# Transposes for the next stage's operand: 32x32 blocks turned on VectorE at full height, quadrants permuted through device memory

## The chip, the core and the metric

The kernel runs on one core of a Trainium2 chip. The metric is device microseconds of one execution, from the first to the last instruction with what the runtime adds around them. TensorE (PE) does matmuls and transposes into PSUM, VectorE (DVE) and ScalarE (ACT) do elementwise work, GpSimd (POOL) some small things, SyncE (SP) starts the loads.

## The reference, cut to what matters

Two layers of an encoder on 256 tokens of width 2048, all in float32. Each layer is three residual steps, each with an RMSNorm ahead:

```
for i in range(2):
    h = h + (even_mixer if i == 0 else odd_mixer)(h, ...)   # norm, projections, attention, projection
    h = h + swiglu(rmsnorm(h), w_gate, w_up, w_down)        # 2048 -> 5632 -> 2048
    h = h + (p[i] @ w_proj) * sigmoid(rmsnorm(h) @ w_pg)    # per-layer embedding
return rmsnorm(h)
```

The even mixer joins a sparse attention over chosen keys with gated linear attention; the odd one is stick-breaking attention with 16 heads of 128. Every product `rmsnorm(h) @ W` contracts over the 2048 columns of `h`, so the 256 tokens of `h` are needed with their columns along the partitions, that is transposed. The same holds for the hidden values of the feed-forward (5632 columns) and for q and k of the odd mixer.

## The kernel before

`h` stays in SBUF as 128 partitions x 2 halves of the tokens x 2048 columns. A product streams its weights once: a unit (`unit`, L176) loads four chunks of 128 rows by 512 columns, 1 MB, in one DMA begun by SP (L184) into one of two `raw` buffers. In two half units each (two chunks), ScalarE casts them to float32r (`whi`, L99), VectorE subtracts to get the low part (`wlo`, L100), each into one of four buffers, and PE does 12 matmuls: for each chunk and each half of the tokens high x high (L201), high x low (L202) and low x high (L203). `block` (L206) runs four units for a contraction of 2048 and leaves two PSUM tiles of 128x512, one for each half of the tokens.

Everything that isn't the stream of weights is put into a list by `later` (L161). `tick` (L169), called after each half unit, takes at most one entry from its front once the entry's delay in half units has gone by and, if it names another entry with `after`, so many half units after that one; `need` (L165) empties the list up to an entry at once. So the order of writing weaves this work into the stream. The framework then plans an order of instructions for each engine from the written order and its own times; in the trace an instruction can stand ahead of one written earlier. Each engine runs its own order strictly, and each queue of DMA issues too.

Three kinds of transposes are in the kernel.

1. The next operand. When a column block of 512 of `h` is final, `finish_cols` (L224) squares it for the norm and puts two calls of `turn_h` (L135) into the list. Each does four 128x128 transposes on PE into a PSUM tile (L141); ScalarE multiplies by the norm's gain and rounds (L146), VectorE forms the low part (L147). The next stage's first block asks for two chunks each with `need`. This happens for five norms, four column blocks each, two calls per block. A sixth norm, the first, is turned while x arrives (`arrive`, L239).
2. The hidden values of the feed-forward (`ffn`, L782): each of 11 blocks of 512 in each of two layers is turned by `turn_blocks` (L123), four list entries of four VectorE transposes each, 32 partitions x 256 columns (L128), into `hx`; then `split_hid` casts (L789) and subtracts (L790).
3. q and k of the odd mixer (`odd_mixer`, L690): the same `turn_blocks`, straight into `qT` and `kT`, four groups of heads, two each. `scores` (L701) then multiplies them on PE (L709, L711); `shares` and `sums` follow.

Other names: `ple` (L847) is the embedding step, `gated` (L861) its sigmoid, product and sum; it begins with four short blocks of two chunks. For the last quarter of the last embedding step `keep` (L892) loads half-wide weights into a buffer of its own (`kept`) and splits them ahead of time. `mixer_out` (L674) is the projection behind a mixer; `square_sum` (L105) writes its squares, which nobody reads, into `sqs`. `stage` (L55) is one buffer for small loads and constants. The final stage sends `h` out (L934).

Of the kernel before, what the change touches and what calls it, by code (L numbers as in the profile page):

```python
# [27 lines left out]
def trunk_kernel(ctx: ExitStack, tc: tile.TileContext, x, p, even_norm, even_w_in, even_w_gk,  # L28
# [36 lines left out]
    # the activation tables and the tensor engine's clock are up when the data comes  # L65
# [7 lines left out]
    # norm gains, one row of 128 per chunk, turned so that a chunk's gains lie along the partitions  # L73
# [29 lines left out]
    ss = {}  # L103

    def square_sum(key, tt, cb, src):  # L105
        if key not in ss:
            ss[key] = sm.tile([P, NT, 4], F32, name="ss")
        scr = sm.tile([P, NB], F32, name="sqs", bufs=1)
        nc.scalar.activation(scr, src, AF.Square, accum_out=ss[key][:, tt, cb:cb + 1])
# [25 lines left out]
    def turn_h(dst, norm, c2):  # L135
        """Chunks 2*c2 and 2*c2+1 of h, transposed, times the gain, split."""
# [39 lines left out]
    def unit(ps, stat, k0, cols, first, last, nk=KU, kw0=None, step=KU, pre=None):  # L176
        """nk chunks of the contraction: cols = [(weight, first column, width)]."""
# [28 lines left out]
    def block(stat, cols, nk=KC, key=None, ps=None, k0=0, k1=None, kw=0, pre=None):  # L206
        """Output columns over chunks k0..k1 of the contraction; returns the two PSUM tiles."""
# [43 lines left out]
    with tc.issue_after(got_gains.ins):  # L251
# [4 lines left out]
    # upb[s, c] = 1/16 where s <= c in one chunk of 64; sub[s, c] = 1/16 where s > c there  # L256
    upb = const.tile([P, P], F32, name="upb")
    nc.gpsimd.memset(upb, 0.0625)
    nc.gpsimd.affine_select(upb, upb, pattern=[[1, P]], compare_op=OP.is_ge, fill=0.0, base=0,
                            channel_multiplier=-1)  # L260
    nc.gpsimd.memset(upb[0:64, 64:128], 0.0)
    sub = stage("sub")[:, :P]
    nc.gpsimd.memset(sub, 0.0625)
    nc.gpsimd.affine_select(sub, sub, pattern=[[-1, P]], compare_op=OP.is_gt, fill=0.0, base=0,
                            channel_multiplier=1)
    nc.gpsimd.memset(sub[64:128, 0:64], 0.0)
    subr = const.tile([P, P], F32R, name="subr")
    nc.vector.tensor_copy(subr, sub)
    # keys no later than the query, in one chunk
    upm = upb.bitcast(I32)  # L270
    # strictly earlier keys, keys along the partitions
# [8 lines left out]
    # -1 where the first index is no earlier than the second  # L280
# [10 lines left out]
    def even_mixer(xs, ps0, ep):  # L291
# [3 lines left out]
        oT = new_act()  # L295

# [12 lines left out]
        def tokens(ps, name, w=NB):  # L309
            """The block's last w columns by tokens, scaled by the row's norm."""  # L310
# [7 lines left out]
        # u0: c (128), the last pair of q_idx (128), k_idx (64), zeros (64), k_idx again (64),  # L318
        # the gate's low-rank part (16), one
# [6 lines left out]
        # c and three pairs of q_idx  # L326
# [8 lines left out]
        # a pair of q_idx, k_idx, w_idx and the gate's low-rank part  # L335
# [71 lines left out]
        def index_heads(pairs, tt):  # L407
            """pairs: [(the pair's columns by tokens, its first head)]"""
# [45 lines left out]
        def choose(tt, n):  # L454
            """Rounds 2n and 2n+1 of eight best each, for 64 in all."""
# [527 lines left out]
```

## Time and profile before

| | |
|---|---|
| time, median of 3 runs | 2442.11 us (2441.62 to 2442.64) |
| span of the profiled execution | 2438.5 us |
| PE busy | 2417.6 us, 99% |
| VectorE busy | 1506.6 us, 62% |
| ScalarE busy | 1154.1 us, 47% |
| GpSimd busy | 19.2 us, 1% |
| weight loads | 447 MB, 184 GB/s over the span |

The span is the profiled execution's own time, from its first to its last instruction. Busy times come from that execution; matmuls overlap, so the time that one adds is read from the starts of its neighbours and not from its own duration. A wait is read from the idle time of an engine just before an instruction and from what ended it.

### The profile page before, as it was taken

The numbers are of one execution on the slowest core, as the hardware profiler recorded it, in microseconds if no ns is written. First come the engines' busy times: TensorE is split into PE (matmuls) and PEld (weight loads), VectorE is DVE, ScalarE is ACT, GpSimd is POOL, SyncE is SP. The second block draws the span as 40 slices with busy tenths as digits, with TensorE's granted clock in tenths as the row PEclk, the third lists the DMA queues.
The fourth block names the chain that finished last, engine by engine and source line by source line (L and its number), as shares of the span: only waits on it lengthen the run. The fifth ranks groups of instructions, "written<-read, shape, count | busy, mean of one in ns | idle before, by whom it ended". The sixth has DMA issues, their size and how long they took to land.

```text
span 2438.5 us, 27647 instructions
## 1 busy us (share of the span) xinstructions
PE 2417.6 (99%) x10966; PEld 1996.5 (82%) x10966; DVE 1506.6 (62%) x1907; ACT 1154.1 (47%) x1418; POOL 19.2 (1%) x45
## 2 busy tenths in 40 slices
PE   8999999999999999999999999999999999999998
PEld 7887788888888888888888888888888888888887
DVE  5765555766756665655676666557667556556564
ACT  6644444344434434446546565544444344444463
POOL 0000000000000000000000000000000000000000
PEclk9999999999999999999999999999999999999999
DMA  6454455566556565555554454555655655556563
GB/s 211 147 169 151 144 194 186 189 196 201 189 192 193 186 205 183 198 190 185 178 190 156 161 184 165 180 190 177 203 190 192 205 190 186 196 187 206 182 231 123
DMA packets 231651, 450.01 MB, mean 185 GB/s; under 512 B 9457, under 2 KB 16337, under 8 KB 231394
## 3 DMA queue, kind: packets, MB, share of 16 engines
q1 hardware_dynamic: 231234, 447.07, 55.6%
q8 instruction: 86, 1.41, 0.2%
q10 hardware_dynamic: 288, 1.18, 0.1%
q14 instruction: 43, 0.35, 0.0%
HBM read 446.12 MB, written 2.10 MB: 184 GB/s over the span
## 4 chain that ended last, share of the span: by engine, by line
PE 91%; issue 5%; ACT 2%; DVE 1%; DMA 1%; SPq 0%; POOLq 0%; POOL 0%; DVEq 0%; ACTq 0%
PE mm L202 29%; PE mm L201 29%; PE mm L203 29%; PE at L141 1%; DVE kT L128 1%; DVE wlo L100 0%; DMA raw<-in_odd_w_in_dram 0%; PE at L424 0%; DMA h<-in_x_dram 0%; PE at L742 0%; DVE sp L719 0%; ACT whi L99 0%; ACT sp L716 0%; ACT sp L715 0%; ACT L715 0%
## 5 line engine op out<-in xcount | busy, mean ns | idle before, releaser
L100 DVE TENSOR_TENSOR wlo<-raw,whi 128x1024 fp32r<-128x1024 f32 (+2 forms) x848 | 1020.7, 1213 | 794.1 <-ACT whi L99 790.1
L99 ACT CAST whi<-raw 128x1024 fp32r<-128x1024 f32 (+2 forms) x848 | 874.8, 1042 | 1053.5 <-PE mm L203 668.8
L201 PE MATMUL mm<-whi,aH 128*128 128x512 f32 (+2 forms) x2656 | 1036.9, 390 | 0.7 <-ACT whi L99 0.7
L202 PE MATMUL mm<-wlo,aH 128*128 128x512 f32 (+2 forms) x2656 | 1028.8, 387 | 4.1 <-DVE wlo L100 4.1
L203 PE MATMUL mm<-whi,aL 128*128 128x512 f32 (+2 forms) x2656 | 1028.7, 387 | 0.0
L202 PEld LDWEIGHTS mm<-wlo,aH 128*128 128x128 f32 x2656 | 499.4, 188 | 104.7 <-DVE wlo L100 5.9
L203 PEld LDWEIGHTS mm<-whi,aL 128*128 128x128 f32 x2656 | 499.1, 188 | 103.4 <-issue 1.0
L201 PEld LDWEIGHTS mm<-whi,aH 128*128 128x128 f32 x2656 | 499.2, 188 | 102.9 <-issue 2.8
L201 PE MATMUL mm<-whi,hH 128*128 128x512 f32 x704 | 277.2, 394 | 0.0
L202 PE MATMUL mm<-wlo,hH 128*128 128x512 f32 x704 | 277.0, 393 | 0.0
L203 PE MATMUL mm<-whi,hL 128*128 128x512 f32 x704 | 273.6, 389 | 0.0
L128 DVE STREAM_TRANSPOSE hx<-sl 32x256 f32<-32x256 f32 x352 | 153.6, 436 | 6.1
L201 PEld LDWEIGHTS mm<-whi,hH 128*128 128x128 f32 x704 | 132.2, 188 | 30.0
L203 PEld LDWEIGHTS mm<-whi,hL 128*128 128x128 f32 x704 | 132.2, 188 | 29.7
L202 PEld LDWEIGHTS mm<-wlo,hH 128*128 128x128 f32 x704 | 132.4, 188 | 26.1
L146 ACT ACTIVATE aH<-at,gT 128x256 fp32r<-128x256 f32 x96 | 45.1, 473 | 51.4 <-DVE aL L147 47.5
L789 ACT CAST hH<-hx 128x1024 fp32r<-128x1024 f32 x22 | 23.2, 1054 | 92.6 <-DVE hx L128 92.6
L147 DVE SCALAR_TENSOR_TENSOR aL<-at,gT,aH 128x256 fp32r<-128x256 f32 x96 | 45.8, 480 | 22.0 <-ACT aH L146 21.9
L234 DVE TENSOR_TENSOR h<-mm,h 128x512 f32<-128x512 f32 x80 | 52.4, 682 | 2.7 <-PE mm L203 2.7
L141 PE MATMUL at<-ident,h 128*128 128x128 f32 x192 | 30.5, 283 | 5.0 <-DMA h<-in_x_dram 5.0
L141 PEld LDWEIGHTS at<-ident,h 128*128 128x128 f32 x192 | 24.9, 145 | 11.8 <-DMA h<-in_x_dram 3.0
L128 DVE STREAM_TRANSPOSE qT<-tok 32x256 f32<-32x256 f32 x64 | 27.9, 436 | 6.8 <-ACT tok L762 5.8
(221 smaller groups left out, 806.8 us busy)
## 6 DMA issues: line engine op xcount, KB each, us to landing
raw<-in_ffn_w_gate_dram SPq DMA_DIRECT2D x88, 1024.0 KB, 5.2
raw<-in_ffn_w_up_dram SPq DMA_DIRECT2D x88, 1024.0 KB, 5.2
raw<-in_ffn_w_down_dram SPq DMA_DIRECT2D x88, 1024.0 KB, 5.0
raw<-in_odd_w_in_dram SPq DMA_DIRECT2D x48, 1024.0 KB, 5.2
raw<-in_even_w_in_dram SPq DMA_DIRECT2D x36, 1024.0 KB, 5.0
raw<-in_ple_w_gate_dram SPq DMA_DIRECT2D x28, 1024.0 KB, 5.1
raw<-in_even_w_out_dram SPq DMA_DIRECT2D x16, 1024.0 KB, 5.1
raw<-in_odd_w_out_dram SPq DMA_DIRECT2D x16, 1024.0 KB, 5.0
```

Source lines behind the costliest of these rows:

```text
L99: nc.scalar.copy(hi, raw)
L100: nc.vector.tensor_tensor(lo, raw, hi.bitcast(F32), OP.subtract)
L128: nc.vector.transpose(dst[32 * a:32 * a + 32, :, :, 32 * q:32 * q + 32], src.rearrange("p t (m a c) -> p t m a c", a=4, c=32)[32 * q:32 * ...
L141: nc.tensor.transpose(ps[:, c, tt, :], h[:, tt, k * P:(k + 1) * P], ident)
L146: nc.scalar.activation(dst[0][:, k, :], src, AF.Copy, scale=g)
L147: nc.vector.scalar_tensor_tensor(dst[1][:, k, :], src, g, dst[0][:, k, :].bitcast(F32), op0=OP.mult, op1=OP.subtract)
L201: nc.tensor.matmul(ps[tt][:, :n], sh, hi[:, c, :n], start=st, stop=False)
L202: nc.tensor.matmul(ps[tt][:, :n], sh, lo[:, c, :n], start=False, stop=False)
L203: nc.tensor.matmul(ps[tt][:, :n], sl, hi[:, c, :n], start=False, stop=en)
L234: nc.vector.tensor_tensor(hs, ps[tt], hs, OP.add)
L789: nc.scalar.copy(d[0], t)
```

## The change

`turn_blocks` is gone; `turn_h` stays for the first norm only. In their place stands `cross`. It turns a block of 256 tokens by 512 columns with one VectorE instruction over all 128 partitions, which transposes each 32x32 block where it lies. Then whole quadrants of 32 partitions must change places with groups of columns. For that four DMAs begun by GpSimd write the four quadrants (32 partitions, 128 KB each, in runs of 1 KB) into a tile in device memory, and two DMAs, also begun by GpSimd, read it back, one for each half of the tokens (128 partitions, 256 KB, in runs of 512 bytes). A read needs all four writes. The tile that comes back, `tx`, has two buffers, so has the one in device memory, and the one between has one.

All five later norms use it: `finish_cols` puts `cross` into the list and two half units behind it two calls of `gain_h`, which multiplies and splits from `tx` as `turn_h` did from PSUM. The feed-forward puts `cross` and, two half units behind it, `split_hid`, which reads `tx` in permuted order. In the odd mixer a ScalarE copy from `tx` into `qT` or `kT` follows two half units behind, and the layout of these two goes by heads.

Room in SBUF is made for it: `sqs` shares the buffer of `stage`; `sgm` is gone, so `gated` writes the sigmoid into its PSUM tile, takes the product into the embedding's tile and adds that; the kept weights are loaded into the two `raw` buffers; the constants `upb` and `subr` move into the even mixer's pool; and `mixer_out` is split in two, so that the pool of `cross` opens when that of the even mixer closes.

```diff
     def square_sum(key, tt, cb, src):
...
-        scr = sm.tile([P, NB], F32, name="sqs", bufs=1)
+        scr = sm.tile([P, NB], F32, name="sqs", tag="stage", bufs=1)
...
-    def turn_blocks(dst, src, a):
...
+    def cross(src):
...
+        tq = pools["x"].tile([P, 4, NT, 4, 32], F32, name="tq", bufs=1)
+        nc.vector.transpose(tq.rearrange("p a t m r -> p t m a r"),
+                            src.rearrange("p t (m a c) -> p t m a c", a=4, c=32))
+        x = pools["x"].tile([P, 8, 4, 32], F32, name="tx")
+        y = pools["y"].tile([4, 32, 4, NT, P], F32, name="ty")
         for q in range(4):
-            nc.vector.transpose(dst[32 * a:32 * a + 32, :, :, 32 * q:32 * q + 32],
-                                src.rearrange("p t (m a c) -> p t m a c", a=4, c=32)[32 * q:32 * q + 32, :, :, a, :])
+            nc.gpsimd.dma_start(y[:, :, q].rearrange("a c t n -> c a (t n)"),
+                                tq[32 * q:32 * q + 32].rearrange("c a t m r -> c a (t m r)"))
+        for t in range(NT):
+            nc.gpsimd.dma_start(x[:, 4 * t:4 * t + 4].rearrange("p q m r -> p q (m r)"),
+                                y[:, :, :, t].rearrange("a c q n -> (a c) q n"))
+        return x
+
+    def crossed(x):
...
+        return x.rearrange("p q m r -> p m q r")
+
+    def flat(t):
...
+        return t.rearrange("p m (q r) -> p m q r", q=8)
...
+    def gain_h(dst, norm, x, c2):
...
+        for k in (2 * c2, 2 * c2 + 1):
+            g = gT[1][:, (norm - 1) * KC + k:(norm - 1) * KC + k + 1]
+            src = crossed(x)[:, k % 4]
+            hi, lo = (flat(d[:, k:k + 1, :])[:, 0] for d in dst)
+            nc.scalar.activation(hi, src, AF.Copy, scale=g)
+            nc.vector.scalar_tensor_tensor(lo, src, g, hi.bitcast(F32), op0=OP.mult, op1=OP.subtract)
...
     def finish_cols(nx, cb):
...
+        x = {}
+        first = (nx["key"], "x", cb)
+        later(lambda: x.update(x=cross(h[:, :, cb * NB:(cb + 1) * NB])), key=first)
         for c2 in (2 * cb, 2 * cb + 1):
-            later(lambda c2=c2: turn_h(nx["dst"], nx["norm"], c2), key=(nx["key"], c2))
+            later(lambda c2=c2: gain_h(nx["dst"], nx["norm"], x["x"], c2), key=(nx["key"], c2), after=(first, 2))
...
-                nc.tensor.matmul(pz[:, 0:256], kT[:, 0, js], qT[:, :, js], start=True, stop=False,
+                nc.tensor.matmul(pz[:, 0:256], kT[:, j, 0:P], qT[:, j, :], start=True, stop=False,
                                  skip_group_check=True)
-                nc.tensor.matmul(pz[:, 256:384], kT[:, 1, js], qT[:, 1, js], start=False, stop=False,
+                nc.tensor.matmul(pz[:, 256:384], kT[:, j, P:], qT[:, j, P:], start=False, stop=False,
                                  skip_group_check=True)
...
-                for a in range(4):
-                    later(lambda t=t, d=dst, a=a: turn_blocks(d.rearrange("p t (m c) -> p t m c", c=P), t, a))
+                x = {}
+                later(lambda t=t, x=x: x.update(x=cross(t)), key=("x3", g, i))
+                later(lambda d=dst, x=x: nc.scalar.copy(flat(d), crossed(x["x"])), after=(("x3", g, i), 2))
                 T.append(dst)
...
-        def split_hid(dst, t, k0):
-            d = [dst[n][:, k0:k0 + 4, :] for n in range(2)]
-            nc.scalar.copy(d[0], t)
-            nc.vector.tensor_tensor(d[1], t, d[0].bitcast(F32), OP.subtract)
+        def split_hid(dst, x, k0):
+            hi, lo = (flat(dst[n][:, k0:k0 + 4, :]) for n in range(2))
+            nc.scalar.copy(hi, crossed(x))
+            nc.vector.tensor_tensor(lo, crossed(x), hi.bitcast(F32), OP.subtract)
...
-                hx = fp.tile([P, 4, NT * P], F32, name="hx")
-                for a in range(4):
-                    later(lambda d=hx, t=sl, a=a: turn_blocks(d.rearrange("p m (t c) -> p t m c", t=NT), t, a))
-                later(lambda t=hx, n=n, gi=gi: split_hid(hT[gi], t, 4 * n), key=("hT", i, b))
+                x = {}
+                later(lambda t=sl, x=x: x.update(x=cross(t)), key=("xT", i, b))
+                later(lambda x=x, n=n, gi=gi: split_hid(hT[gi], x["x"], 4 * n), key=("hT", i, b),
+                      after=(("xT", i, b), 2))
...
-            sgm = pp.tile([P, NB], F32, name="sgm", bufs=2)[:, :w]
-            nc.scalar.activation(sgm, pg[:, :w], AF.Sigmoid, scale=rs[:, tt:tt + 1])
-            nc.vector.tensor_tensor(sgm, sgm, eb[c0 // NB][tt][:, c0 % NB:c0 % NB + w], OP.mult)
...
+            nc.scalar.activation(pg[:, :w], pg[:, :w], AF.Sigmoid, scale=rs[:, tt:tt + 1])
+            e = eb[c0 // NB][tt][:, c0 % NB:c0 % NB + w]
+            nc.vector.tensor_tensor(e, pg[:, :w], e, OP.mult)
             hs = h[:, tt, c0:c0 + w]
-            nc.vector.tensor_tensor(hs, hs, sgm, OP.add)
+            nc.vector.tensor_tensor(hs, hs, e, OP.add)
...
-            raw = pp.tile([P, KU, HB], F32, name="kept", bufs=1)
+            raw = wp.tile([P, KU, NB], F32, name="raw", bufs=2)[:, :, :HB]
```

## Rows read from the trace of the kernel before

**Rows 1.** which engine is busy; the page's line 1, busy us, share, instructions

```profile
span 2438.5 us, 27647 instructions
PE 2417.6 (99%) x10966; PEld 1996.5 (82%) x10966; DVE 1506.6 (62%) x1907; ACT 1154.1 (47%) x1418; POOL 19.2 (1%) x45
```

**Rows 2.** busy time by windows: the first feed-forward, the odd mixer

```profile
440.00:1080.00 640.00, 640.00 (x2816) 528.34 (x2816) 399.86 (x460) 266.64 (x269) 0.00 (x0) 1.00 0.59 194
1215.00:1560.00 345.00, 341.14 (x1561) 283.12 (x1560) 229.88 (x332) 195.70 (x244) 0.70 (x1) 1.00 0.52 172
```

**Rows 3.** waits of PE, the longest one that isn't at the start

```profile
PE mm L202 <- DVE wlo L100: 4.1, 5, 0.8
```

**Rows 4.** PE in order of time around one call of turn_h: start, us, instruction

```profile
1082.46 0.39 PE L203 MATMUL mm<-whi,hL 128*128 128x512 f32 x1
1082.69 0.60 PE L141 MATMUL at<-ident,h 128*128 128x128 f32 x4
...
1083.60 0.39 PE L203 MATMUL mm<-whi,hL 128*128 128x512 f32 x1
...
1084.28 0.39 PE L203 MATMUL mm<-whi,hL 128*128 128x512 f32 x1
```

**Rows 5.** groups by line and shape: count, busy us, mean ns, idle before

```profile
L100 DVE TENSOR_TENSOR wlo<-raw,whi 128x1024 fp32r<-128x1024 f32 x832 | 1010.4, 1223 | 779.8 <-ACT whi L99 775.9
L99 ACT CAST whi<-raw 128x1024 fp32r<-128x1024 f32 x832 | 865.5, 1050 | 1040.2 <-PE mm L203 661.2 <-DMA raw<-in_ffn_w_up_dram 152.9 <-DMA raw<-in_odd_w_in_dram 68.9
...
L128 DVE STREAM_TRANSPOSE hx<-sl 32x256 f32<-32x256 f32 x352 | 153.6, 436 | 6.1
...
L146 ACT ACTIVATE aH<-at,gT 128x256 fp32r<-128x256 f32 x96 | 45.1, 473 | 51.4 <-DVE aL L147 47.5 <-PE at L141 3.9
...
L141 PE MATMUL at<-ident,h 128*128 128x128 f32 x192 | 30.5, 283 | 5.0 <-DMA h<-in_x_dram 5.0
...
L733 DVE TENSOR_TENSOR at<-at,diagb 128x256 f32<-128x256 f32 x16 | 6.4, 423 | 0.0
...
L667 POOL TENSOR_TENSOR sg<-sg,gn 128x512 f32<-128x512 f32 x4 | 5.1, 1294 | 5.9 <-ACT sg L665 5.9
```

**Rows 6.** DMA issues: count, KB each, median us from issue to landing

```profile
raw<-in_ffn_w_gate_dram SPq DMA_DIRECT2D x88, 1024.0 KB, 5.2
...
kept<-in_ple_w_gate_dram SPq DMA_DIRECT2D x4, 512.0 KB, 6.0
...
out_dram<-h SPq DMA_DIRECT2D x8, 256.0 KB, 2.8
...
praw<-in_p_dram SPq DMA_DIRECT2D x2, 256.0 KB, 5.1
```

**Rows 7.** SP in order of time, one issue: start, us

```profile
2343.85 0.37 SPq L894 DMA_DIRECT2D kept<-in_ple_w_gate_dram  x1
```

**Rows 8.** all engines in order of time, end of the first embedding step

```profile
1212.27 1.05 ACT L99 CAST whi<-raw 128x1024 fp32r<-128x1024 f32 x1 [1.66 <-PE mm L203]
...
1214.27 1.37 ACT L864 ACTIVATE sgm<-mm,rstd 128x512 f32<-128x512 f32 x2 [0.94 <-PE mm L203]
...
1216.28 1.29 DVE L867 TENSOR_TENSOR h<-h,sgm 128x512 f32<-128x512 f32 x2
```

**Rows 9.** the same, odd mixer, from the end of k to its scores

```profile
1259.30 1.31 ACT L762 ACTIVATE tok<-mm,rstd 128x512 f32<-128x512 f32 x2 [0.54 <-PE mm L203]
...
1260.64 3.57 DVE L128 STREAM_TRANSPOSE kT<-tok 32x256 f32<-32x256 f32 x8 [0.62 <-ACT tok L762]
...
1276.05 0.59 PE L709 MATMUL at<-qT,kT 128*128 128x256 f32 x2
```

**Rows 10.** ScalarE in order of time, last embedding step

```profile
2349.24 1.04 ACT L99 CAST wh<-kept 128x1024 fp32r<-128x1024 f32 x1
2353.91 2.01 ACT L99 CAST whi<-raw 128x1024 fp32r<-128x1024 f32 x2 [3.62 <-DMA raw<-in_ple_w_gate_dram]
...
2358.59 1.05 ACT L99 CAST wh<-kept 128x1024 fp32r<-128x1024 f32 x1
```

More of the change, by code (lines that the diff above doesn't have):

```diff
@@ L121, in rstd_of @@
         return rstds[key]
-    def turn_blocks(dst, src, a):
-        for q in range(4):
-            nc.vector.transpose(dst[32 * a:32 * a + 32, :, :, 32 * q:32 * q + 32],
-                                src.rearrange("p t (m a c) -> p t m a c", a=4, c=32)[32 * q:32 * q + 32, :, :, a, :])
+    pools = {}
+    def cross(src):
[4 more added lines that the diff above has]
+        y = pools["y"].tile([4, 32, 4, NT, P], F32, name="ty")
+        for q in range(4):
+            nc.gpsimd.dma_start(y[:, :, q].rearrange("a c t n -> c a (t n)"),
[8 more added lines that the diff above has]
+        return t.rearrange("p m (q r) -> p m q r", q=8)
     def new_act():
@@ L253, in trunk_kernel @@
     done.update((("n0", i), 0) for i in range(KC // 2))
[L257 to L270, printed above, removed]
     diag = const.tile([P, P], F32, name="diag")
@@ L295, in even_mixer @@
         oT = new_act()
+        upb = ep.tile([P, P], F32, name="upb", bufs=1)
+        nc.gpsimd.memset(upb, 0.0625)
+        nc.gpsimd.affine_select(upb, upb, pattern=[[1, P]], compare_op=OP.is_ge, fill=0.0, base=0,
+                                channel_multiplier=-1)
+        nc.gpsimd.memset(upb[0:64, 64:128], 0.0)
+        sub = stage("sub")[:, :P]
+        nc.gpsimd.memset(sub, 0.0625)
+        nc.gpsimd.affine_select(sub, sub, pattern=[[-1, P]], compare_op=OP.is_gt, fill=0.0, base=0,
+                                channel_multiplier=1)
+        nc.gpsimd.memset(sub[64:128, 0:64], 0.0)
+        subr = ep.tile([P, P], F32R, name="subr", bufs=1)
+        nc.vector.tensor_copy(subr, sub)
+        upm = upb.bitcast(I32)
         def t2(name, dt=F32):
@@ L623, in outputs @@
             for a in range(2):
-                scr = sm.tile([P, NB], F32, name="sqs", bufs=1)
+                scr = sm.tile([P, NB], F32, name="sqs", tag="stage", bufs=1)
                 nc.scalar.activation(scr[:, :256], ov[g][:, tt, a * 256:(a + 1) * 256], AF.Square,
@@ L672, in even_mixer, with mixer_out_first, mixer_out @@
         return oT
-    def mixer_out(oT, W, nx):
+    def mixer_out_first(oT, W):
         for i in range(4):
             need(("oT", i))
-        part = {}
-        for cb in range(2):
-            part[cb] = block(oT, [(W, cb * NB, NB)], k1=8)
+        part = [block(oT, [(W, cb * NB, NB)], k1=8) for cb in range(2)]
         for i in range(4, 8):
             need(("oT", i))
+        return part
+    def mixer_out(oT, W, nx, part):
         for cb in range(4):
-            ps = block(oT, [(W, cb * NB, NB)], ps=part.get(cb), k0=8 if cb < 2 else 0)
+            ps = block(oT, [(W, cb * NB, NB)], ps=part[cb] if cb < 2 else None, k0=8 if cb < 2 else 0)
             add_to_h(ps, cb)
@@ L758, in odd_mixer @@
                     nc.vector.tensor_scalar(rq, rs, float(128 ** -0.5), None, op0=OP.mult)
-                dst = op.tile([P, NT, NB], F32, name="qT" if i == 0 else "kT")
+                dst = op.tile([P, 4, NT * P], F32, name="qT" if i == 0 else "kT")
                 t = op.tile([P, NT, NB], F32, name="tok")
@@ L885, in squared @@
             c0, w = parts[n]
-            scr = sm.tile([P, NB], F32, name="sqs", bufs=1)
+            scr = sm.tile([P, NB], F32, name="sqs", tag="stage", bufs=1)
             nc.scalar.activation(scr[:, :w], h[:, tt, c0:c0 + w], AF.Square, scale=float(D ** -0.5),
@@ L939, in trunk_kernel @@
         nx = start_norm("n1", 1)
-        mixer_out(oT, even_w_out[0], nx)
+        part = mixer_out_first(oT, even_w_out[0])
+    pools["x"] = ctx.enter_context(tc.tile_pool(name="xp", bufs=2))
+    pools["y"] = ctx.enter_context(tc.tile_pool(name="yp", bufs=2, space=bass.MemoryType.DRAM))
+    mixer_out(oT, even_w_out[0], nx, part)
     with tc.tile_pool(name="fp0", bufs=2) as fp:
@@ L950, in trunk_kernel @@
         nx = start_norm("n4", 4)
-        mixer_out(oT, odd_w_out[0], nx)
+        mixer_out(oT, odd_w_out[0], nx, mixer_out_first(oT, odd_w_out[0]))
     with tc.tile_pool(name="fp1", bufs=2) as fp:
```

## The prediction

> **What bounds the kernel now.** I read the busy shares first, then the windows, then the waits. TensorE (PE) is busy 2417.6 of 2438.5 us [rows 1]. Two of its phases are in the windows: in 440 to 1080 us, all feed-forward, it is busy 640.00 of 640 us with 2816 matmuls, so one starts every 0.227 us; in the odd mixer (1215 to 1560) it idles 3.9 us [rows 2]. PE's own waits say the same: the longest group, for the low halves of the weights, is 4.1 us in all [rows 3]. So what counts is (a) work taken off PE, and (b) waits that come to stand in PE's order. VectorE (62%) and ScalarE (47%) matter only through (b). One half unit of weights is 12 matmuls, 12 x 0.227 = 2.73 us; I use it as a clock. The median, 2442.1, is 3.6 us above the span of the profiled execution, and I keep that 3.6.
>
> **The change part by part.**
>
> *Transposes leave PE.* Of the 48 calls of `turn_h`, eight are for the first norm and stay; five norms x 8 = 40 go, with four transposes each. Their 283 ns apiece overlap and are no price [rows 5]. The price is what the matmuls slip: around one call, from the L203 at 1082.46 to the next L203 at 1083.60 is 1.14 us, while three steps without transposes (1083.60 to 1084.28) take 0.68 [rows 4]. So a call costs 0.46 us of PE, and 40 give 18.2 us. PE is full there, so this comes off the end: **-18.2**.
>
> *VectorE.* Gone are 480 transposes of 32x256 (30 blocks x 16) at 436 ns, 209 us [rows 5]. Each of 50 crossings (20 for norms, 8 in the odd mixer, 22 in the feed-forwards) adds one of 128x1024. No such one is in the trace. A 32x256 one takes about what a two-input instruction of 128x256 takes (423 ns), and a two-input one of 128x1024 takes 1223 ns; bounds 1.2 and 4 x 0.436 = 1.74 us; I take 1.23, as the 256-wide shapes agree [rows 5]. VectorE ends 148 us less busy. Nothing waits for it but in the odd mixer, where its stretches of transposes delay the weights' low halves; of the 3.9 us idle there [rows 2] I give back **-2** (bounds 0 and -3.9). ScalarE gets eight copies of 128x1024 more, 1.05 us each like its casts [rows 5].
>
> *The chain of a crossing.* Transpose, four writes of 128 KB begun by GpSimd, a wait of its queue for all four, two reads of 256 KB, arrival. GpSimd starts no DMA in the trace, so I bound by other queues' rows: 256 KB of output reach memory in 2.8 us, 256 KB in rows of 1 KB arrive in 5.1 us, 512 KB of them in 6.0 [rows 6]. For an issue I take 0.4 us, as SP takes (0.37 [rows 7]); GpSimd's longest instructions, 1.29 us [rows 5], are the other end. Middle: 1.23 + 4 x 0.4 + 2.8 + 2 x 0.4 + 5.1 = 11.5 us. High: 1.74 + 4 x 1.3 + 2.8 + 2 x 1.3 + 6.0 = 18.3. Low: 1.2 + 1.6 + 1.4 + 0.8 + 2.8 = 7.8, each write being half of the output's row and a read as quick as that.
> The Trainium skill ("DMA: Bandwidth & Descriptors", Anatomy of one DMA — SWDGE path) gives a DMA begun by GpSimd about 2.0 us plus its bytes at 436 GB/s; by it, estimated, write and read would land in 2.3 and 2.6 us and the chain would take 8.5 us; the sum would be 1.7 us lower. The trace of before has no such DMA to hold against it.
>
> *Who waits for it: next stages.* The last column block's crossing must be back when PE comes to chunk 12 of the next stage, 6 half units (16.4 us) on. Before the odd mixer the block's products end by 1214.27, h is whole at 1216.28 + 1.29 = 1217.57 [rows 8], VectorE has a weight half in between (1.22), so the crossing starts at 1218.8 and lands at 1230.3; the gain (0.47 [rows 5]) and the split after it add 1.0, and PE comes there at 1230.6: 0.7 us late. At the high chain 7.5 us. Before both feed-forwards there is no sigmoid and product (2.0 us from the first sigmoid to the first sum [rows 8]): in time at the middle, 5.5 us late each at the high end. The two embedding stages begin with four short blocks (10.9 us), so nothing is late. Sum **+0.7** (bounds 0 and 18.5).
>
> *Who waits for it: the odd mixer's scores.* k's products end by 1259.30, its 16 transposes begin at 1260.64, and PE takes up the scores at 1276.05 [rows 9]. The written order lets them come 5 half units (13.7 us) behind the products, at 1273.0; the crossing would land at 1260.64 + 11.5 = 1272.1 and its copy end at 1273.2: 0.2 us late. Four groups make **+1** (bounds 0 and 4 x 7 = 28).
>
> *Who waits for it: ScalarE and VectorE.* Behind the gain and split of a crossing stand the weight splits, which feed PE. There are four half-unit buffers: a buffer freed by PE is wanted 3 x 2.73 = 8.2 us later, and cast and subtraction take 1.05 + 1.22 [rows 5], so 5.9 us of waiting are free. The planner doesn't keep the written order (casts of coming halves stand ahead of the sigmoid [rows 8]), so a wait is the chain's length beyond what it plans for, and I cost it at **0** (bounds 0 and, at 0.7 us for each of the 50, 35). Extra traffic is 50 x 1 MB beside 450 MB, on transfer engines busy 0.59 of that feed-forward window [rows 2]; a weight load landing in 7 instead of 5.2 us [rows 6] is hidden by the same buffers.
>
> *The kept weights share the stream's two buffers.* In four units of the last stage a half-wide load takes one of them. A load holds its buffer 5.2 us and then for two splits (about 3.4 us), a kept one 6.0 + 2.3 [rows 5, 6]: 16.9 us of two buffers, 8.4 us a unit where PE needs 5.45. Four such units fall 12 us back, of which the buffers cover 5.9 at most; but ScalarE already waits 3.6 us for loads here and two kept casts stand 9.4 us apart, not 5.45 [rows 10], which softens it. I take **+4** (bounds 0 and 9).
>
> *Small things.* The squares' scratch shares one buffer with the gains' and the constants' staging: the gains' load, which SP has in line ahead of weights, waits for the squares and two constants: **+1** (0 to 3). Sigmoid into PSUM and product from there: nothing, since PE has its next products in line; only the last one lies in the tail, where it takes the place of a like one. The new places of two constants: nothing.
>
> Sum: -18.2 - 2 + 0.7 + 1 + 4 + 1 = -13.5. 2438.5 - 13.5 + 3.6 = **2428.6**, say 2429.
>
> **The rivals.**
> 1. *The crossing stands ahead of the splits on ScalarE for longer than the buffers hold (slower).* For it: four writes, then two reads that can't be begun before, and nothing in the trace shows what a planner thinks of them. If it placed the splits just 5.45 us behind the transposes, the middle chain would wait 6.1 us, 0.2 over what is free; with a chain of 12.4 us, 1.1 over, which on 42 crossings outside the odd mixer is 46 us: 2429 + 46 = 2475. Against it: the order is planned, and over half of VectorE's load of transposes goes. It decides the sign once a crossing loses over 13.5 / 50 = 0.27 us. With 0.7 us each the time is 2464. Chance 0.25.
> 2. *PE gets its time back as waits at stage starts and scores (no change).* With a chain of 14.5 us: 3.7 before the odd mixer, 2 x 1.7 before the feed-forwards, 4 x 3.2 for the scores, 19.9 in place of 1.7: 2447; with 13 us, 2437. Chance 0.13. For it: in both places PE has nothing else in line. Against: the scores may be planned later, as they were.
> 3. *GpSimd's issues wait for VectorE (no change).* If each of the six can begin only when the instruction under way on VectorE has ended, it waits at most 1.22 us [rows 5], on average half of that in the busy half of the time: the chain grows by about 2 us, to 13.5, and the time becomes 2440. Against it: what fills VectorE has two inputs and runs at 1223 ns for 1024 columns and 423 for 256 [rows 5], one column per 1.04 ns, no doubled rate that a second port could give. Chance 0.04.
> The Trainium skill has the rule ("SBUF — State Buffer", SBUF: two separate sides): a VectorE instruction in a mode that takes both ports locks GpSimd out while it would write descriptors. By it the trace's rate speaks for no such lock here.
> 4. *All waits stay hidden and the odd mixer's idle time goes:* 2442.1 - 18.2 - 3.9 = 2420. Part of the forecast.
>
> **How the numbers follow.** Forecast (2420 to 2437, with rival 4) 0.58, rival 2 0.13, rival 3 0.04, rival 1 0.25. A measurement can tell about 0.2% (5 us) from no change, so faster means under 2437.2 and slower over 2447: 0.58, 0.17 (rivals 2 and 3) and 0.25. The range of 8 in 10 goes from 2419 to 2458: it takes in rivals 2 and 3 and of rival 1 all that loses up to 0.6 us a crossing (29 / 50), which leaves out 0.14 above and 0.03 below. The forecast's own range is 2420 to 2437.
>
> **What would show it.** Right: matmuls of 128x128 against `ident` from h are 32 instead of 192; PE busy near 2400 us, its waits still a few us; VectorE near 1360. From transpose to arrival 9 to 13 us. Wrong: PE waiting for `whi` or `wlo` by tens of us with ScalarE's wait on `tx` in front (rival 1); PE waiting at chunk 12 or at L709's line for `aH` or `kT` (rival 2); `wh` casts in the last 100 us with PE idle beside them (the kept weights over 9 us). A chain over 14 us would make the prediction wrong by itself.

## The result, and the profile after

The changed kernel takes 2468.86 us (median of 4 executions, 2466.48 to 2475.51) beside 2442.38 of the kernel before on the same chip: ratio 1.0115, 95% interval 1.0100 to 1.0129. It is slower, where 2429 was forecast with a range up to 2458. The profiled execution has a span of 2464.8 us, 26.3 more than before.

The page of the changed kernel: busy time of PE and GpSimd, GpSimd's two issuing lines (busy us, mean ns), and the landing times.

```profile
PE 2415.7 (98%) x10806; PEld 1989.0 (81%) x10806; DVE 1355.3 (55%) x1477; ACT 1162.6 (47%) x1426; POOL 206.5 (8%) x345
...
L135 POOL DMA_DIRECT2D ty<-tq x200 | 110.0, 559 | 1545.7 <-DVE tq L130 1405.0
...
L138 POOL DMA_DIRECT2D tx<-ty x100 | 75.2, 756 | 308.9 <-DMA ty<-tq 271.5
...
ty<-tq POOLq DMA_DIRECT2D x200, 128.0 KB, 5.3
tx<-ty POOLq DMA_DIRECT2D x100, 256.0 KB, 3.4
```

Against [rows 1], PE has 160 instructions fewer, as meant, but is only 1.9 us less busy, and that in a longer span: it idles 49.1 us where it idled 20.9, and parts of its work run slower. Its waits say for what (line, releaser, us in total, times, longest):

```profile
PE mm L229 <- ACT whi L99: 9.1, 4, 4.4
PE mm L229 <- DVE h L265: 7.6, 2, 4.3
...
PE at L742 <- ACT kT L798: 4.8, 4, 2.1
PE mm L229 <- ACT aH L175: 4.2, 3, 2.6
PE mm L230 <- DVE wlo L100: 3.9, 6, 0.9
PE mm L229 <- ACT pe L890: 3.3, 1, 3.3
```

Before, the row for `wlo` stood at 4.1 [rows 3] and the one for `whi` at this:

```profile
PE mm L201 <- ACT whi L99: 0.7, 2, 0.5
```

The others are new. Where they lie, by windows (us, PE busy, PEld, DVE, ACT, POOL; then the granted clock, the DMA share and GB/s):

```profile
400.00:410.00 10.00, 7.44 (x27) 5.60 (x26) 6.49 (x8) 5.69 (x9) 1.54 (x2) 0.86 0.73 248
440.00:1080.00 640.00, 640.00 (x2816) 528.36 (x2815) 338.63 (x302) 268.90 (x267) 38.46 (x62) 1.00 0.65 212
1110.00:1120.00 10.00, 5.68 (x23) 4.39 (x22) 5.08 (x7) 3.28 (x5) 1.50 (x2) 0.86 0.75 237
1120.00:1130.00 10.00, 10.00 (x37) 7.83 (x36) 5.94 (x10) 7.70 (x15) 4.62 (x7) 0.80 0.85 283
1230.00:1240.00 10.00, 5.14 (x22) 3.75 (x21) 4.21 (x5) 3.99 (x4) 1.54 (x2) 0.83 0.91 330
...
2340.00:2350.00 10.00, 6.75 (x18) 5.00 (x18) 3.62 (x8) 5.79 (x13) 4.60 (x7) 0.70 0.68 241
...
2370.00:2420.00 50.00, 43.27 (x166) 33.46 (x164) 28.52 (x30) 24.39 (x31) 0.00 (x0) 0.90 0.55 190
```

In the feed-forward window nothing is lost: 2816 matmuls in 640 us, as before [rows 2], though ten crossings run in it. What is lost lies at five stage starts (400, 1115, 1235, 1625 and 2335 us) and at the end of the last stage (2380 to 2420), and behind most of these stalls (not behind that at 1625) the granted clock falls to between 0.70 and 0.87: part of that time is spent at 1.2 in place of 2.4 GHz. In sums over windows of 10 us, 1 minus the clock makes 20.1 us, against 2.2 before, some of it while PE idles anyway. So the ledger is: 18.2 gained by the prediction's price of a call, 28.2 more idle, and 26.3 + 18.2 - 28.2 = 16.3 us that are left for work at the lower clock.

One crossing, the last block before the first feed-forward, in the timeline (start, us):

```profile
391.15 1.25 DVE L130 STREAM_TRANSPOSE tq<-h 128x1024 f32<-128x1024 f32 x1
392.32 1.18 DVE L100 TENSOR_TENSOR wlo<-raw,whi 128x1024 fp32r<-128x1024 f32 x1
392.70 2.20 POOL L135 DMA_DIRECT2D ty<-tq  x4 [11.86 <-DVE tq L130]
400.92 1.54 POOL L138 DMA_DIRECT2D tx<-ty  x2 [4.90 <-DMA ty<-tq]
405.10 1.71 ACT L175 ACTIVATE aH<-tx,gT 128x256 fp32r<-128x256 f32 x4 [0.96 <-DMA tx<-ty]
```

From transpose to gain 13.95 us, where the middle of the forecast was 11.5: the transpose and the reads are no longer than was taken, the issues and the wait for the writes are. And this is the shortest of the fifty: from the start of the transpose to the landing of the last read they take 13.9 to 17.0 us, 14.6 in the median. The landings of this crossing's first and third write (KB, us):

```profile
ty<-tq POOLq DMA_DIRECT2D x1, 128.0 KB, 2.3
ty<-tq POOLq DMA_DIRECT2D x1, 128.0 KB, 6.2
```

Over all crossings the four writes land in 2.4, 3.7, 6.4 and 6.4 us in the median, in their order. The page's 5.3 is the middle of these unlike ones. In 46 of the 50 crossings SyncE begins two loads of weights between the first write and the first read.

The stall before the first embedding stage, as the chain of waits tells it (start, us, what):

```profile
1109.19 6.51 DMA raw<-in_ple_w_proj_dram
...
1115.78 1.05 ACT whi L99
...
1116.86 0.07 DVE wlo L100
...
1118.00 0.69 DVE h L265
...
1118.83 0.77 PE mm L229
```

From this load on no tile of a crossing stands in it. A load of 512 KB for the stage's short blocks takes 6.51 us (in this stretch their median landing is 5.3, before 3.7), the split waits for it, VectorE's addition of the feed-forward's last block (L265) stands behind that split, and PE can't have the PSUM tile until it is done. What PE does then, in its timeline:

```profile
1118.83 0.77 PE L229 MATMUL mm<-whi,pH 128*128 128x512 f32 x1 [4.32 <-DVE h L265]
1119.40 0.63 PE L230 MATMUL mm<-wlo,pH 128*128 128x512 f32 x1
1119.82 0.63 PE L231 MATMUL mm<-whi,pL 128*128 128x512 f32 x1
```

After 4.3 us of idling the same matmuls start every 0.43 us, not every 0.227.

### The profile page after: what moved, and what is told of

The parts are those of the page before. It is cut to its first block, busy times and chain, and to the rows that moved or that the text cites. A ratio compares the mean times of both kernels' runs of the same rounds, so it can differ in the third digit from the quotient of the medians.

```text
span 2464.8 us, 27530 instructions
## 1 busy us (share of the span) xinstructions
PE 2415.7 (98%) x10806; PEld 1989.0 (81%) x10806; DVE 1355.3 (55%) x1477; ACT 1162.6 (47%) x1426; POOL 206.5 (8%) x345
## 4 chain that ended last, share of the span: by engine, by line
PE 78%; DMA 11%; DVE 4%; ACT 3%; issue 2%; POOL 1%; SPq 0%; DVEq 0%; POOLq 0%; ACTq 0%
PE mm L230 25%; PE mm L229 25%; PE mm L231 25%; DMA ty<-tq 3%; DVE wlo L100 2%; DMA tx<-ty 2%; DMA raw<-in_odd_w_in_dram 2%; ACT whi L99 1%; DMA raw<-in_ffn_w_down_dram 1%; DMA raw<-in_ple_w_gate_dram 1%; DMA raw<-in_even_w_out_dram 1%; DMA raw<-in_odd_w_out_dram 1%; DVE tq L130 1%; DVE h L265 1%; POOL ty L135 1%
## 5 line engine op out<-in xcount | busy, mean ns | idle before, releaser
L135 POOL DMA_DIRECT2D ty<-tq x200 | 110.0, 559 | 1545.7 <-DVE tq L130 1405.0
L230 PEld LDWEIGHTS mm<-wlo,hH 128*128 128x128 f32 x704 | 132.4, 188 | 26.3
L138 POOL DMA_DIRECT2D tx<-ty x100 | 75.2, 756 | 308.9 <-DMA ty<-tq 271.5
L265 DVE TENSOR_TENSOR h<-mm,h 128x512 f32<-128x512 f32 x80 | 51.3, 682 | 0.0
L175 ACT ACTIVATE aH<-tx,gT 128x256 fp32r<-128x256 f32 x80 | 34.3, 498 | 23.4 <-DMA tx<-ty 17.0
L176 DVE SCALAR_TENSOR_TENSOR aL<-tx,gT,aH 128x256 fp32r<-128x256 f32 x80 | 33.7, 481 | 12.6 <-ACT aH L175 12.6
L109 ACT ACTIVATE sqs<-h 128x512 f32<-128x512 f32 x48 | 30.3, 632 | 14.7 <-DVE h L265 11.2
L824 DVE TENSOR_TENSOR hL<-tx,hH 128x1024 fp32r<-128x1024 f32 x22 | 27.0, 1225 | 16.1 <-ACT hH L823 15.8
L833 ACT ACTIVATE sl<-mm,rstd 128x512 f32<-128x512 f32 x44 | 29.4, 686 | 9.8 <-PE mm L231 9.6
```

The source lines that it names most:

```text
L135: nc.gpsimd.dma_start(y[:, :, q].rearrange("a c t n -> c a (t n)"), tq[32 * q:32 * q + 32].rearrange("c a t m r -> c a (t m r)"))
L138: nc.gpsimd.dma_start(x[:, 4 * t:4 * t + 4].rearrange("p q m r -> p q (m r)"), y[:, :, :, t].rearrange("a c q n -> (a c) q n"))
L175: nc.scalar.activation(hi, src, AF.Copy, scale=g)
L176: nc.vector.scalar_tensor_tensor(lo, src, g, hi.bitcast(F32), op0=OP.mult, op1=OP.subtract)
L230: nc.tensor.matmul(ps[tt][:, :n], sh, lo[:, c, :n], start=False, stop=False)
L265: nc.vector.tensor_tensor(hs, ps[tt], hs, OP.add)
```

## The experiments

**1. Kept weights in a buffer of their own.** Line 927, alone:

```
-            raw = wp.tile([P, KU, NB], F32, name="raw", bufs=2)[:, :, :HB]
+            raw = pools["x"].tile([P, KU, HB], F32, name="kept", tag="tq", bufs=1)
```

> The changed kernel with one thing undone: the kept weights of the last step have a buffer of their own again (the idle one between transpose and write). Theory A (the shared buffers stop PE late in the kernel: 6.7 us idle between 2380 and 2420 us of the changed kernel's trace, and a granted clock of 0.83, 0.87 and 0.79 in three of the 10-us windows there, which is 5 us of lost work): about 2457 us, no idle PE there. Theory B (the stream is late there because of the crossings before): no change, 2466 to 2470.

Measured: 2453.75 us (2451.31 to 2456.81), 1.0052 of before (1.0037 to 1.0067). 15.1 us are back. The end of the last stage is whole again:

```profile
1110.00:1120.00 10.00, 5.50 (x18) 4.09 (x17) 5.10 (x7) 4.56 (x8) 3.10 (x5) 0.71 0.74 259
...
2370.00:2420.00 50.00, 50.00 (x222) 41.43 (x221) 32.90 (x36) 27.65 (x36) 0.00 (x0) 1.00 0.62 208
```

222 matmuls in these 50 us against 166 in the changed kernel: 56 x 0.227 = 12.7 us. The embedding stage's stall stays.

**2. Norms transposed on PE again**, by `turn_h`; crossings only in the feed-forwards and the odd mixer; kept weights as in the change.

```
-        later(lambda: x.update(x=cross(h[:, :, cb * NB:(cb + 1) * NB])), key=first)
...
+            later(lambda c2=c2: turn_h(nx["dst"], nx["norm"], c2), key=(nx["key"], c2))
```

> The changed kernel with the five norms turned by PE through PSUM again; crossings only for feed-forward and odd mixer (30 of 50). Theory A (all the loss at stage starts is that of the 20 norm crossings: 20.6 us idle and 12 us by the clock, and the PE transposes are worth 18.2): 2468.9 - 32.6 + 18.2 = 2454.5, with the idle time in the last step left. Theory C (every crossing costs about the same, 27 us / 50): 2468.9 - 20 x 0.9 + 18.2 = 2469.

Measured: 2456.03 us, 1.0064 (1.0049 to 1.0079).

**3. The other way round**: crossings only for the 20 blocks of the norms, the feed-forwards and the odd mixer by `turn_blocks` as before.

> The other half: crossings only for the 20 norm blocks; feed-forward and odd mixer turn with 16 small VectorE transposes per block as before. Theory A (the 30 others cost nothing): 2466 to 2471. Theory C (27 us of idle time spread over all 50, with the clock 0.9 us each): 2468.9 - 30 x 0.9 = 2442.

Measured: 2470.94 us, 1.0125 (1.0110 to 1.0141). All of the loss is there without the 30 crossings of the feed-forwards and the odd mixer.

**4. Edits 1 and 2 together.**

> Norms turned by PE and kept weights in their own buffer; crossings for feed-forward and odd mixer alone. Theory A: both losses are gone and so is the gain: 2440 to 2445, as the kernel before. Theory C: 2457.

Measured: 2444.34 us (10 executions), 1.0010 (1.0000 to 1.0020). So the 30 crossings outside the norms cost at most some 5 us; this profile's idle is 3.6 us over before's, and PE's wait for `kT` at the odd scores, 7.6 us in four, is the only long one left. Sharing the kept weights' buffers costs 15.1 (1 against the change) or 11.7 us (4 against 2). The norms' crossings take off 18.2 us of transposes and yet make the kernel 2453.75 - 2444.34 = 9.4 us slower: they bring about 27.6 us of loss.

What of this is waiting (W) and what is transfers in each other's way (T)? Two runs, both with the kept weights' own buffer.

**5. The norms' crossings made and not used**, the operands turned on PE:

```
+        later(lambda: cross(h[:, :, cb * NB:(cb + 1) * NB]))
         for c2 in (2 * cb, 2 * cb + 1):
+            later(lambda c2=c2: turn_h(nx["dst"], nx["norm"], c2), key=(nx["key"], c2))
```

> The kernel of the fourth experiment (norms transposed on PE, kept weights in their own buffer; 2444 us), and in addition the 20 crossings of the norm blocks are made as in the change, but nothing reads what they bring: their transpose on VectorE, their six transfers and GpSimd's issues are there, the instructions that wait for them are not. W (the stage starts lose their time because ScalarE and VectorE stand in line behind a crossing that has not landed): 2444 to 2448, no PE wait over 1.5 us and no fall of the granted clock at 400, 1115, 1235, 1625 and 2335 us. T (they lose it because the crossing's transfers hold up the loads of weights): as the first experiment plus the 18 us that the transposes cost PE, 2460 to 2472, with the stalls of 2 to 5 us at these places still there.

Measured: 2453.23 us (2450.16 to 2453.35), 1.0050 (1.0034 to 1.0067), 8.9 over experiment 4: between the two. Its windows at the embedding stages:

```profile
1110.00:1120.00 10.00, 9.44 (x44) 7.16 (x43) 6.70 (x9) 5.37 (x12) 1.50 (x2) 1.00 0.76 240
1120.00:1130.00 10.00, 8.67 (x42) 6.78 (x42) 5.46 (x9) 7.41 (x14) 3.92 (x7) 1.00 0.61 214
2330.00:2340.00 10.00, 9.58 (x45) 7.33 (x44) 5.25 (x7) 4.42 (x8) 1.50 (x2) 1.00 0.74 237
2340.00:2350.00 10.00, 8.68 (x40) 6.40 (x39) 3.75 (x8) 6.34 (x13) 3.61 (x6) 1.00 0.86 320
```

Traffic and VectorE's transposes make PE idle 3.6 us there, in small pieces with no fall of the clock, and at no other stage start. (The profiled execution, 2450.16, is 5.3 over that of experiment 4.) That the long stalls need the waiting as well is not shown by it: PE makes its transposes again here, and four calls of 0.46 us bring it 1.8 us later to the first embedding stage's short blocks, with as much more room for the loads. The load of the third short block takes 6.1 us here too, but it begins 6.0 us ahead of PE's first matmul of these blocks (1107.3 and 1113.33 us); in the changed kernel it is 2.4 (1109.19 and 1111.61).

**6. The last of each norm's four blocks on PE**, three by crossing:

```
+        if cb == 3:
+            for c2 in (2 * cb, 2 * cb + 1):
+                later(lambda c2=c2: turn_h(nx["dst"], nx["norm"], c2), key=(nx["key"], c2))
+            return
```

> The changed kernel with the kept weights in their own buffer, and of each norm's four column blocks the last one transposed on PE, the first three by a crossing (15 crossings in place of 20; 30 of the 40 calls of turn_h gone, 13.8 us by the 0.46 us of the prediction). W: only the last block's crossing is late, as the first three have one to three more blocks of products behind them: the stalls at the stage starts go and the time is 2444 - 14 = 2430, up to 2434, faster than before. T, or a loss that each norm crossing brings by itself (about 1.4 us each for 20 of them): three quarters of the stalls stay, 2446 to 2452.

Measured: 2453.45 us, 1.0049 (1.0034 to 1.0064). The number is nearest to T's (up to 2452); the places are not. At 400 and 1625 us PE no longer idles at all, at the odd mixer 2.2 us, but at the embedding stages 3.7 and 6.4 us with the clock down to 0.83 and 0.66. W's step that only the last block is late holds for the feed-forwards and fails for the embedding stages. From this came a third theory, P: what is lost depends on the place, and most of it lies before the embedding stages.

**7 and 8. P tested by two kernels**, odd mixer and feed-forwards by `turn_blocks`, kept weights in their own buffer. Seven has crossings for the norms of the feed-forwards and the odd mixer, first three blocks only; eight has them for the two embedding norms, all four blocks:

```
+        if not (nx["norm"] in (1, 3, 4) and cb < 3):      # 7;  8: nx["norm"] in (2, 5)
+            for c2 in (2 * cb, 2 * cb + 1):
+                later(lambda c2=c2: turn_h(nx["dst"], nx["norm"], c2), key=(nx["key"], c2))
+            return
```

> Crossings only for the norms of both feed-forwards and of the odd mixer, and there only for the first three column blocks (9 of 50); everything else by TensorE and by quadrants as before, kept weights in their own buffer. 18 calls of turn_h leave PE, 8.3 us. P (the loss sits in two places: the last block of a norm, which must be back at once, and the two embedding stages, whose short blocks want many loads just when four crossings run): 2441.4 - 8.3 and up to 2 us for the wait at the odd mixer, 2433 to 2436, faster than before. Q (each norm crossing costs the like wherever it is, 27.6 us lost on 20 in the first experiment, 1.4 us each): 2441.4 - 8.3 + 9 x 1.4 = 2445.7.

> Crossings only for the norms of the two embedding stages, all four blocks (8 of 50); everything else as in the run beside it. 16 calls of turn_h leave PE, 7.4 us. P: the stalls of the first experiment at 1110 to 1130 us (4.9 us idle, 3.4 us of clock) and at 2330 to 2360 us (6.6 and 3.4) come whole, 18.3 us: 2441.4 - 7.4 + 18.3 = 2452. Q: 8 x 1.4 us come, 2445.

Measured: seven 2435.94 us (10 executions), 0.9982 (0.9973 to 0.9991); eight 2453.04, 1.0054 (1.0037 to 1.0071); the kernel before 2440.49 beside both. P gave 2433 to 2436 and 2452, Q 2446 and 2445. The same operation saves time in one place and costs it in the other. Eight's windows:

```profile
1110.00:1120.00 10.00, 5.29 (x20) 3.96 (x19) 5.10 (x7) 3.54 (x6) 1.75 (x3) 0.84 0.74 246
1120.00:1130.00 10.00, 10.00 (x38) 8.06 (x37) 5.17 (x7) 7.45 (x13) 4.57 (x7) 0.82 0.88 284
...
2340.00:2350.00 10.00, 8.24 (x24) 6.03 (x24) 4.59 (x8) 8.54 (x17) 3.78 (x6) 0.72 0.69 230
```

In 1120 to 1130 us PE is busy throughout and yet makes 38 matmuls, where 44 fit at 0.227 us. Seven has no such window; its one wait of the crossings' kind is 2.0 us at the odd mixer for the last block, which its PE must now turn as soon as h is whole. 18 x 0.46 = 8.3 less 2.5 of idle and 0.5 of clock makes 5.3, the medians differ by 4.6. It beats the kernel before by under two parts in a thousand, and with it the changed one.

**9 and 12. Does a stall cost more than its length?** In the kernel before, twelve times in the feed-forwards, a chain of GpSimd instructions starts when a low half is ready, and a small transpose that PE has in line waits for it (7 to 12 instructions in the one, 3 to 6 in the other):

```
+            for m in range(HOLD.get(state["unit"], 0)):
...
+                nc.gpsimd.tensor_tensor(held, held if m else lw[:, 0], held if m else lw[:, 1], OP.mult)
+                if m + 1 == HOLD[state["unit"]]:
+                    nc.tensor.transpose(at_tile()[:, :P], held[:, :P], ident)
```

> The kernel before, with twelve stalls of PE in the feed-forwards: a chain of 7 to 12 GpSimd instructions of about 1.3 us starts when a low half is ready, some 8 us before PE wants it, and a small transpose that PE has in line ahead of that half's matmuls waits for the chain. Idle times of about 1 to 7.5 us each, twice. K (a long stall costs more than its length, as the granted clock falls after it): after stalls of over about 2.5 us the granted clock is 0.83 or lower in the next 10 us and about 2 to 3.5 us more are lost for each, so the time is 2441 plus the idle time plus about 20 us. L (the clock falls at the stage starts for another reason, for instance that matmuls of half width run there): the clock stays at 1.00 behind all twelve and the time is 2441 plus the idle time, about 50 us.

> The kernel of the ninth experiment with shorter chains: 3, 4, 5 and 6 GpSimd instructions, three of each, for stalls of PE of about 1.5 to 5.5 us, the sizes that the changed kernel has at its stage starts (seven instructions gave 6.6 us). K: behind the stalls of over about 2.5 us the granted clock shows 0.83 or lower in one or two windows of 10 us, behind the shorter ones 1.00; the time is 2441 plus the idle time (about 40 us) plus 5.7 us for the twelve transposes plus 1.5 to 2 us for each stall with a fall (6 to 9 of them), about 2500. L (the falls in the changed kernel are bound to the places, and those of the ninth experiment to stalls of over 6 us): the clock stays at 1.00 behind all of them and the time is 2441 plus idle time plus 5.7.

Measured, one execution each: 2575.29 and 2488.28 us. The stalls of nine came out longer than meant, 6.6 to 10.9 us, 108 in all, and the clock fell behind every one. The span grew by 134.7, and the twelve made transposes have a price of their own, which a stall without a fall in twelve shows:

```profile
896.85 0.39 PE L211 MATMUL mm<-whi,hL 128*128 128x512 f32 x1
898.12 0.33 PE L199 MATMUL at<-ident,held 128*128 128x128 f32 x1 [0.89 <-POOL held L197]
...
898.52 0.39 PE L210 MATMUL mm<-wlo,hH 128*128 128x512 f32 x1
```

From 896.85 to 898.52 is 1.67 us; less two steps of 0.227 and the idle 0.89, a transpose adds 0.33 (the 5.7 us of the expectation, 0.47 each, are too much). So 134.7 - 108.2 - 4.0 = 22.5 us are the clock's; K had put 20. In twelve, ten stalls are left, PE idles 33.4 us more than before, the span grew by 47.7, and 47.7 - 33.4 - 4.0 = 10.3 us remain for the clock (8.5 against the execution of the kernel before that ran beside it). Its windows, two of the stalls:

```profile
630.00:640.00 10.00, 7.85 (x36) 6.20 (x35) 6.74 (x5) 5.25 (x6) 6.13 (x4) 1.00 0.62 210
640.00:650.00 10.00, 10.00 (x39) 8.11 (x38) 2.47 (x3) 2.94 (x3) 0.00 (x0) 0.83 0.31 111
...
2080.00:2090.00 10.00, 7.00 (x32) 5.50 (x31) 5.75 (x4) 3.15 (x3) 5.07 (x4) 1.00 0.56 187
2090.00:2100.00 10.00, 10.00 (x46) 8.29 (x45) 4.52 (x4) 3.81 (x4) 0.00 (x0) 1.00 0.37 136
```

The clock fell behind the stalls of 2.15, 4.1, 5.5, 6.4 and 7.4 us and not behind those of 0.9, 1.1, 1.7, 1.7 and 3.0. So the stall, not the place, brings the fall (K); for stalls of 2 to 3 us it goes either way, here as in the experiments above.

**10 and 11. The six transfers begun by SyncE, by ScalarE**, nothing else (`nc.gpsimd.dma_start` becomes `nc.sync` or `nc.scalar`).

> The changed kernel with the six transfers of each crossing begun by SyncE in place of GpSimd, nothing else. If the queue is of no matter (M): SyncE's issue takes 0.37 us against 0.56 and 0.76 on GpSimd, so the chain is 6 x 0.37 = 2.2 in place of 3.7 us of issue, 1.5 us shorter, the stalls at the stage starts shrink with it, 2455 to 2465. If what is queued behind a waiting issue decides (N): the reads wait some 5 us for the writes at the head of SyncE's line, and the loads of weights stand behind them; with two load buffers each of 50 crossings loses about 2 to 5 us of loads and some of it reaches PE: over 2500.

> The same with ScalarE beginning them. M: 2455 to 2465. N: the reads wait at the head of ScalarE's line for the writes, some 5 us, and the casts of weights stand behind; ScalarE is busy 47% and has 5.9 us free per crossing, so less than with SyncE at most of the 50, more at the stage starts: 2475 to 2550.

Measured, one execution each: 2486.4 and 2509.02 us beside 2441.11. Both are slower than with GpSimd. With SyncE the page's landings and SyncE's waits are:

```profile
ty<-tq SPq DMA_DIRECT2D x200, 128.0 KB, 2.4
tx<-ty SPq DMA_DIRECT2D x100, 256.0 KB, 4.3
...
SPq L135 <- DVE tq L130: 227.6, 50, 7.6
SPq L138 <- DMA ty<-tq: 94.7, 88, 3.3
```

The writes land in 2.4 us, not 5.3, a crossing's transfers are back 10.6 us after the start of its transpose in the median, not 14.6 (with ScalarE 14.2), and still the time is longer: SyncE stands 322 us for crossings with the loads of weights behind it, and PE's wait for `whi` grows from 9.1 to 29.0 us. That is N's mechanism, though its number for SyncE was too high; ScalarE's lies in N's range. That the chain is shorter is not worth what is queued behind its waits.

## Why the prediction was wrong

Step by step, in the prediction's order.

*Transposes leave PE, -18.2: right*, though 40 x 0.46 is 18.4. Six, seven and eight add up with 0.46 us a call: idle time, clock and this term make seven -5.3 (the medians differ by -4.6), and the wait before the embedding stages is the only thing that sends eight the other way.

*VectorE and the odd mixer's idle time, -2: size wrong.* VectorE went from 62% to 55% and its transpose of 128x1024 takes 1.25 us, as taken. But PE idles 4.8 us at the odd scores, where it idled 3.9: the waits there now end on `kT`'s copy.

*The chain, 11.5 us: term mis-sized, 14.6.* Issues take 0.56 and 0.76, not 0.4; reads land in 3.4, not 5.1. One write alone lands sooner than the 2.8 that was taken, the first of four in 2.4; but the last, which the reads need, lands in 6.4. Experiment 10 has all four in 2.0 to 2.9 us, in their order's medians, but there only one load begins between the first write and the first read, so it doesn't part the queue from the traffic. The page cited in the prediction (the Trainium skill, "DMA: Bandwidth & Descriptors", Anatomy of one DMA — SWDGE path) gives an estimate of 2.3 and 2.6 us for a write and a read; the first write agrees, the last ones and the reads (3.4) don't, and the measurement decides. A chain over 14 us was named as what would make the prediction wrong, and that sign came; but 10, with a chain 4 us shorter and a longer time, shows that its length alone doesn't decide.

*Next stages, +0.7 (0 to 18.5): the step that failed.* Experiment 4 against 1 puts the whole of the norms' loss at 27.6 us. Of this, the feed-forwards and the odd mixer follow the reasoning: at 400 and 1625 us PE waits 2.6 and 1.2 us for the last block's gain, at 1235 it waits 4.4 for a half of weights (with a chain of 14.5 us rival 2 had 1.7, 1.7 and 3.7), and with that block on PE (6, 7) the stall goes or shrinks to 2. "The two embedding stages begin with four short blocks (10.9 us), so nothing is late" is the sentence that fell. It asked only when PE needs the crossing. It did not ask what the stream of weights does while four crossings run. The chain of waits ahead of the stall shows it (start, us, what):

```profile
1082.02 7.11 DMA raw<-in_ffn_w_down_dram
...
1091.43 1.29 DVE h L265 x2
...
1095.13 6.93 DMA raw<-in_ffn_w_down_dram
```

A load, the cast and the split behind it, in VectorE's order the addition to h, then the crossing's transpose (1.25 us), and behind that the split that frees the buffer for the next load: one round takes 13.1 us, where PE makes a column block's 48 matmuls in 10.9. The loads of 1 MB at this place land in 6.6 us in the median, before in 4.9. So the stream falls back block by block, until the third short block's load begins 2.4 us ahead of PE's first short matmul in place of 6.6 (before: 1106.28 and 1112.90), lands in 6.51 in place of 3.7, and the addition that gives PE its PSUM tile back stands behind its split. ScalarE waited for no crossing's tile on this way, from 1075 to 1118 us. Eight alone shows the place: the eight crossings there lose 2453.04 - 2440.49 + 7.4 = 20 us.

*Odd scores, +1: small, as put.* The four waits for `kT` sum to 4.8 us, 0.9 more than the idle time of before; with the -2 above, -1 was forecast for this stage and +0.9 came.

*ScalarE and VectorE in order, 0 (0 to 35): right in the feed-forwards, wrong at stage ends.* Ten crossings cost nothing in those 640 us, so the four half-unit buffers cover them, and rival 1 with its price per crossing is wrong, though its sign came. At the second embedding stage the first gain on ScalarE (L175) stood 6.4 us, with the squares and the copies of `pe` behind it, for which PE waited 3.3. The profile puts the end of those 6.4 us down to a matmul, which reads neither `tx` nor `aH`; the crossing's second read, begun at 2335.54, landed at 2342.79, and the gain began at 2342.88. In eight, at the same place, the profile names the read itself:

```profile
2340.77 0.91 ACT L180 ACTIVATE aH<-tx,gT 128x256 fp32r<-128x256 f32 x2 [5.71 <-DMA tx<-ty]
```

In the changed kernel that read took 7.2 us, beside a load of 512 KB that took 8.4 and one of 1 MB for the last norm's gain that took 6.7.

*Kept weights, +4 (0 to 9): term mis-sized, 12 to 15.* The working had 8.4 us a unit against PE's 5.45, and ScalarE's casts of the weights that come with a kept half do stand 8.5 us apart:

```profile
2388.17 1.99 ACT L99 CAST whi<-raw 128x1024 fp32r<-128x1024 f32 x2 [5.57 <-DMA raw<-in_ple_w_gate_dram]
...
2396.69 2.00 ACT L99 CAST whi<-raw 128x1024 fp32r<-128x1024 f32 x2 [5.58 <-DMA raw<-in_ple_w_gate_dram]
```

Its 12 us less the 5.9 that the buffers cover are 6.1, and PE idles 6.7 in 2370 to 2420. Taking 4 instead, because some waiting was there before [rows 10], was the smaller mistake; the larger is the clock, 0.90 in that window, which makes 5.0 us more of the 12.7.

*The clock: in no term.* 16.3 us of the 26.3, by the ledger above; by 9 and 12 a stall that is followed by a fall costs about 2 us beyond its length in the mean (22.5 / 12 = 1.9, 10.3 / 5 = 2.1), and seven stalls of the changed kernel are followed by one. Both ends of all wait terms lacked it.

The rivals: 2 had the place (stage starts) with too low a price, 2437 to 2447, as it left out the embedding stages and the clock. 3 was not tried by a run; in the crossing shown the four issues follow each other in 2.20 us while VectorE runs a split (392.32), so no issue waited for VectorE there. Of the range, the upper end left out that the kept weights and the stage starts could both go over their bounds.

How the 20 us at the embedding stages divide is not settled. The trace shows three parts: loads that take longer beside the crossings, splits that stand behind transposes and gains in the engines' orders, and at the second stage a gain that waits for its crossing. A fourth is that PE, without its transposes, comes sooner; 5 gave it these back, so it doesn't tell them apart. (Of 5's 8.9 us its profile holds only 5.3, and these windows 3.6.) No run gave the stream a third load buffer or began the crossings at another moment.

## What to carry to other kernels

Cost a detour through memory where its data is wanted, and also by what runs beside it at that moment: the same crossing was free inside the feed-forwards, saved 0.25 us for each `turn_h` that it replaced before them and the odd mixer (4.6 / 18), and cost 2.5 us of stalls each before the embedding stages. Follow the wait on: the late load, the split behind it, and the addition behind the split that holds PE's tile. To a stall of PE of several us add its price in clock, here about 2 us. And take the length of a chain from the last of its transfers to land, not from the median of all.

## What was not expected of the hardware

Stalls of PE of 4 to 5 us are followed by matmuls at the 1.2 GHz level, one every 0.43 us in place of 0.227, for a stretch that showed as a granted clock of 0.66 to 0.87 in windows of 10 us; of the stalls of about 2 to 3 us some were followed by such a stretch and some not (2.15 was and 3.00 was not, both in experiment 12), and of the made ones below 1.8 us none was.

Of four writes of 128 KB to device memory that GpSimd began 0.56 us apart, the first landed in 2.4 us and the third and fourth in 6.4 (medians of fifty). The medians over all writes, 5.3 us with GpSimd, 3.1 with ScalarE and 2.4 with SyncE, don't compare the engines: with SyncE one load of weights begins between a crossing's first write and first read, with GpSimd two in 46 of 50. A 256 KB read landed in 3.4, 4.5 and 4.3 us. GpSimd took 0.56 and 0.76 us to begin one, SyncE 0.37 for a weight's load [rows 7]. VectorE's 32x32-block transpose of 128x1024 takes 1.25 us, near a two-input instruction of that size (1.22).
